# Weight tiles of the 256-column products placed alternately 64 and 192 bytes past the activations

## The chip, the core and the metric

The kernel runs on one core of one Trainium2 chip. The metric is the device time of one execution in microseconds (us), median of three runs; shorter is better. The core has a matrix engine (TensorE, in the profile PE for the products and PEld for the loads of their stationary operand), a vector engine (DVE), a scalar engine (ACT), a general engine (POOL, nearly unused here) and a queue that issues transfers (SP). All of them read and write an on-chip memory of 128 partitions. An address below is the byte offset in each partition, and only its remainder mod 256 matters to the change.

## The reference, cut to what matters

The reference is one layer of a decoder on 256 tokens of width 2048. It has two parts, and each ends in a layer norm of the residual sum:

```
h = layer_norm(x) * (1.0 + sc1) + sh1
y = token_mixer(h, w_in, ...)          # attention and mLSTM, merged, then @ w_o
x = layer_norm(ALPHA * x + g1 * y, ln_g[0], ln_b[0])
h = layer_norm(x) * (1.0 + sc2) + sh2
y = conv_ffn(h, w_up, ...)             # (silu(conv(h @ w_up[a])) * (h @ w_up[g])) @ w_down
x = layer_norm(ALPHA * x + g2 * y, ln_g[1], ln_b[1])
```

What matters for the change are two of the matrix products: `h @ w_in` for the part of the columns that is wanted transposed (3072 columns), and `h @ w_up` (2048 by 11264), the largest product of all.

## The kernel before, in words

Every large product is made of three products of split numbers. An fp32 weight tile `w` (128 x 1024) is loaded by the SP queue, ACT rounds it into `wh` (line 117), DVE forms the remainder `wl = w - wh` (line 118), and TensorE sums high times high, high times low and low times high. `wh` and `wl` come from a ring of four buffers each.

There are two forms. In the a-form (`mm_a`, lines 131 to 135) a block of activations is the stationary operand and the weights are streamed past it, 512, 392 or 256 columns at a time. In the b-form (`mm_b`, lines 125 to 129) a 128 x 128 block of the weight tile is the stationary operand, and 256 columns of activations (`hT` or `h2T`, high and low part) are streamed past it. Each product loads its stationary block anew, while the product before it is streaming. A weight tile of the b-form therefore gives 8 blocks and 24 products of 256 columns.

The b-form is used in two places:

- in the projection stage, by the stream `wb` over `w_in_b` (48 tiles, 1152 products, PSUM name `ps_b`). The contraction is cut into four groups of 3, 4, 5 and 4 blocks of 128 rows (`GROUPS`), so that the first products can start early. After the b-form products of a group come its a-form products (`ps_a`).
- in `up` (lines 1095 to 1117), over `w_up`: 44 values of `j`, each with four tiles (`b` for the two halves of the columns, `hf` for the two halves of the contraction), 176 tiles and 4224 products, PSUM name `ps_up`. The first 22 values of `j` run before the first half of the down projection, the other 22 after it.

TensorE takes its instructions in the order of the program; outside three short stretches that order is a scheduler's. `load_split(src, off)` takes a tile from each ring that is 1088 numbers wide (1024 + `OFFN`), and uses 1024 of them from number `off` on. A tile has 4352 bytes, 17 times 256, so that all four buffers have the same remainder, and `off` alone sets where the weights begin mod 256. The activations `hT` and `h2T` begin at remainder 0, and so does each block of 256 columns in them.

```
OFFB, OFFA, OFFN = 16, 48, 64      # line 41, in numbers of 4 bytes
```

Before, every b-form tile begins at number 16, 64 bytes past the remainder of the activations. The 256-column products of the a-form (in `proj_rows`, for `w_o` and `w_down`) use `OFFA`, 48 numbers or 192 bytes; there the weights are the streamed operand and the activations the stationary one, so that the stationary operand again begins 64 bytes (256 - 192) past the streamed one. The wider a-form products use no offset.

Of the kernel before, what the change touches and what calls it, by code (L numbers as in the profile page):

```python
# [14 lines left out]
P = 128  # L15
# [22 lines left out]
WB = (7, 4, 4)  # L38
NU0, NU1 = 4, 1
WARM = 20  # L40
OFFB, OFFA, OFFN = 16, 48, 64
MORD = (0, 2, 1, 3)
PTV = 2
YA = 2
# [1 line left out]
AW = 392  # L46
# [8 lines left out]
def build(ctx: ExitStack, tc: tile.TileContext, d, out, dbg=None):  # L55
# [36 lines left out]
    def t2(shape, name, dt=F32):  # L92
        return p0.tile(shape, dt, name=name, tag="t2", bufs=NT2)

    def bank(pool, name, dt=F32):
        return pool.tile([P, 512], dt, name=name, tag="b")

    def load(src):
        n = src.shape[-1]
        t = wp.tile([P, 1024], F32, name="w", tag="w", bufs=WB[0])  # L100
        nc.sync.dma_start(t[:, :n], src)
        return t
# [8 lines left out]
    def load_split(src, off=0):  # L111

        n = src.shape[-1]
        t = load(src)
        wh = wp.tile([P, 1024 + OFFN], F32R, name="wh", tag="wh", bufs=WB[1])[:, off:off + 1024]
        wl = wp.tile([P, 1024 + OFFN], F32R, name="wl", tag="wl", bufs=WB[2])[:, off:off + 1024]
        nc.scalar.copy(wh[:, :n], t[:, :n])  # L117
        lows.append(nc.vector.tensor_sub(wl[:, :n], t[:, :n], wh[:, :n]))  # L118
        return wh, wl
# [5 lines left out]
    def mm_b(ps, wh, wl, i, xt, k, start, stop):  # L125
        a, b = wh[:, i * P:(i + 1) * P], wl[:, i * P:(i + 1) * P]
        mm(ps, a, xt[:, k, 0, :], start, False)
        mm(ps, a, xt[:, k, 1, :], False, False)
        mm(ps, b, xt[:, k, 0, :], False, stop)
# [362 lines left out]

    def stream(src, width, per, off=0):

        tiles = iter(range(src.shape[0]))
        while True:
            wh, wl = load_split(src[next(tiles)][:, :width * per], off)
            work()
            for i in range(per):
                yield wh[:, i * width:(i + 1) * width], wl[:, i * width:(i + 1) * width]  # L500

    wb, wa, wv = (stream(d[n], w, p, o) for n, w, p, o in (("w_in_b", P, 8, OFFB), ("w_in_a", AW, 2, 0),
                                                           ("w_in_v", 512, 2, 0)))
    k0 = 0
    for gi, kn in enumerate(GROUPS):
        nxt = gi < len(GROUPS) - 1
# [7 lines left out]
        def work():  # L514
            if comp and next(comp[0], 1) is None:
                return
            comp.clear()
            tk.tick(rate)

        for b in range(NBLK):  # L520
            if b % 2 == 0:
                ps = bank(psm, "ps_b")
            for k in range(k0, k0 + kn):
                wh, wl = next(wb)
                mm_b(ps[:, (b % 2) * S:(b % 2 + 1) * S], wh, wl, 0, hT, k, k == k0, k == k0 + kn - 1)
            if b % 2 == 1:
                dst, kind = dest_b(b // 2)
                src = (ps.rearrange("p (w t k) -> p w t k", w=2, t=2) if kind
                       else ps.rearrange("p (a b) -> p a b", a=2))
# [9 lines left out]
        for c in range(6):  # L539
            pss = [bank(psm, "ps_a%d" % t) for t in range(2)]  # L540
            aw = AW if c < 4 else 512
            for k in range(k0, k0 + kn):
                wh, wl = next(wa if c < 4 else wv)
# [4 lines left out]
            for t in range(2):  # L548
                dst, src = projA[:, t, c * AW:(c + 1) * AW], pss[t][:, :aw]
                if c >= 4:  # L550
                    dst = mv1[:, t, 2 * c - 8:2 * c - 6, :MDV]
                    src = src.rearrange("p (h v) -> p h v", v=MDV)
# [469 lines left out]
    with tc.manual_schedule(engines={mybir.EngineType.DVE, mybir.EngineType.Activation}):  # L1022
# [33 lines left out]
        for p in range(8):  # L1056
# [8 lines left out]
            for i in range(2):  # L1065
                k = 2 * p + i
                src = pss[p // 2, i][:, (p % 2) * S:(p % 2 + 1) * S]
# [27 lines left out]
    def up(j):  # L1095

        ps = bank(psm, "ps_up")
        for b in range(2):
            for hf in range(2):
                wh, wl = load_split(d["w_up"][j * 4 + b * 2 + hf], OFFB)  # L1100
                for k in range(8):
                    mm_b(ps[:, b * S:(b + 1) * S], wh, wl, k, h2T, hf * 8 + k, hf == 0 and k == 0,
                         hf == 1 and k == 7)
                tk.tick(UR)
        a, gate = ps[:, :S], ps[:, S:]
        fw = lambda i: ffn[:, 3 * j + i:3 * j + i + 1]
        av = t2([P, S], "av")
        nc.scalar.activation(av, a, AF.Identity, bias=ffn[:, R_FB + j:R_FB + j + 1], scale=fw(2))
        for i in (1, 0):
            sh = 2 - i  # L1110
            nc.vector.scalar_tensor_tensor(av[:, sh:], a[:, :S - sh], fw(i), av[:, sh:],
                                           op0=ALU.mult, op1=ALU.add)
        nc.scalar.activation(av, av, AF.Silu)
        nc.vector.tensor_mul(av, av, gate)
        u = uTt[:, j % KH]
        nc.scalar.copy(u[:, 0, :], av)
        nc.vector.tensor_sub(u[:, 1, :], av, u[:, 0, :])

    for j in range(KH):
        up(j)  # L1120
        if j == 2:
            for c in range(2):
                tk.add(ada_rows(5, g2, c))
# [3 lines left out]
    for j in range(KH, KF):  # L1127
        up(j)
# [147 lines left out]
```

## Time and profile before

| what | value |
|---|---|
| median of 3 runs | 1485.79 us (1484.89, 1485.79, 1488.66) |
| the profiled execution, its own time | 1490.49 us |
| its span, first to last instruction | 1488.5 us |
| mean granted TensorE clock | 0.989 |
| TensorE busy (products) | 1439.5 us, 97% of the span |
| loads of stationary operands busy | 1304.1 us, 88% |
| DVE busy, ACT busy | 1072.4 us (72%), 710.0 us (48%) |
| DMA queue of the loads | 74.1% of the 16 engines' span |

A product is busy from its start until its last result, and the next one starts before that, so neighbouring products overlap. What a product costs in a dense stretch is therefore not its duration but the distance from one start to the next, called its pitch here. It is read from a timeline, where the starts stand, or from the number of products in a stretch that holds nothing else.

### The profile page before, as it was taken

The numbers are of one execution on the slowest core, as the hardware profiler recorded it, in microseconds if no ns is written. First come the engines' busy times: TensorE is split into PE (matmuls) and PEld (weight loads), VectorE is DVE, ScalarE is ACT, GpSimd is POOL, SyncE is SP. The second block draws the span as 40 slices with busy tenths as digits, with TensorE's granted clock in tenths as the row PEclk, the third lists the DMA queues.
The fourth block names the chain that finished last, engine by engine and source line by source line (L and its number), as shares of the span: only waits on it lengthen the run. The fifth ranks groups of instructions, "written<-read, shape, count | busy, mean of one in ns | idle before, by whom it ended". The sixth has DMA issues, their size and how long they took to land.

```text
span 1488.5 us, 24079 instructions
## 1 busy us (share of the span) xinstructions
PE 1439.5 (97%) x9470; PEld 1304.1 (88%) x9470; DVE 1072.4 (72%) x1565; ACT 710.0 (48%) x954; POOL 2.1 (0%) x6
## 2 busy tenths in 40 slices
PE   5999999999999999999699999999999999999997
PEld 4998998877667888888699999998899999999886
DVE  7899887888777798678867767755555555555566
ACT  5654443637764444435544444443334444444341
POOL 0000000000000000000000000000000000000000
PEclk9999999999999999999799999999999999999998
DMA  9999897885868999999078868866666666665661
GB/s 354 349 348 349 312 326 265 316 314 187 284 224 287 326 317 326 340 333 331 25 259 276 280 229 281 281 188 194 196 200 187 185 188 190 187 185 187 195 205 65
DMA packets 104081, 374.81 MB, mean 252 GB/s; under 512 B 11680, under 2 KB 12192, under 8 KB 103200
## 3 DMA queue, kind: packets, MB, share of 16 engines
q1 hardware_dynamic: 103968, 373.27, 74.1%
q8 instruction: 74, 1.21, 0.3%
q14 instruction: 39, 0.32, 0.1%
HBM read 371.13 MB, written 2.10 MB: 251 GB/s over the span
## 4 chain that ended last, share of the span: by engine, by line
PE 88%; DVE 6%; DMA 3%; ACT 2%; issue 1%; SPq 0%; DVEq 0%; ACTq 0%
PE ps_up L90 33%; PE ps_d L90 16%; PE ps_mg L90 10%; PE ps_b L90 7%; PE ps_br L90 6%; PE ps_a L90 6%; PE ps_o L90 5%; DVE wl L118 1%; DVE w L181 1%; PE ps_y L90 1%; DMA w<-in_w_in_b_dram 1%; DMA w<-in_w_in_v_dram 1%; ACT wh L117 1%; DVE xz L950 1%; DVE xz L955 1%
## 5 line engine op out<-in xcount | busy, mean ns | idle before, releaser
L118 DVE TENSOR_TENSOR wl<-w,wh 128x1024 fp32r<-128x1024 f32 (+1 forms) x478 | 576.3, 1206 | 350.3 <-ACT wh L117 348.4
L117 ACT CAST wh<-w 128x1024 fp32r<-128x1024 f32 (+1 forms) x478 | 495.3, 1038 | 657.3 <-PE ps_up L90 206.3
L90 PE MATMUL ps_up<-h2T,wh 128*128 128x256 f32 x2816 | 501.1, 282 | 0.5 <-DVE h2T L1077 0.3
L90 PEld LDWEIGHTS ps_up<-h2T,wh 128*128 128x128 f32 x2816 | 433.9, 189 | 1.0 <-DVE h2T L1077 0.5
L90 PE MATMUL ps_up<-h2T,wl 128*128 128x256 f32 x1408 | 396.3, 281 | 0.0
L90 PEld LDWEIGHTS ps_up<-h2T,wl 128*128 128x128 f32 x1408 | 268.0, 190 | 0.1
L181 DVE SCALAR_TENSOR_TENSOR w<-w,crow 128x1024 f32<-128x1024 f32 x192 | 233.6, 1219 | 1.1 <-DMA w<-in_w_ada_dram 1.1
L90 PE MATMUL ps_d<-wh,uTt 128*128 128x512 f32 (+1 forms) x792 | 209.8, 353 | 0.0
L90 PE MATMUL ps_mg<-wh,hT 128*128 128x512 f32 x512 | 169.9, 403 | 0.0
L90 PEld LDWEIGHTS ps_d<-wh,uTt 128*128 128x128 f32 x792 | 139.8, 188 | 20.7
L90 PE MATMUL ps_d<-wl,uTt 128*128 128x512 f32 (+1 forms) x396 | 139.8, 353 | 0.0
L90 PE MATMUL ps_b<-hT,wh 128*128 128x256 f32 x768 | 135.9, 282 | 2.7 <-ACT wh L117 2.7
L90 PEld LDWEIGHTS ps_b<-hT,wh 128*128 128x128 f32 x768 | 117.2, 190 | 7.2 <-issue 3.7
L90 PEld LDWEIGHTS ps_mg<-wh,hT 128*128 128x128 f32 x512 | 96.1, 188 | 23.5 <-issue 4.1
L90 PE MATMUL ps_a<-wh,hT 128*128 128x392 f32 (+1 forms) x384 | 110.6, 363 | 2.4 <-ACT wh L117 2.4
L90 PE MATMUL ps_b<-hT,wl 128*128 128x256 f32 x384 | 106.0, 281 | 0.6 <-DVE wl L118 0.5
L90 PE MATMUL ps_mg<-wl,hT 128*128 128x512 f32 x256 | 99.9, 390 | 0.0
L90 PEld LDWEIGHTS ps_d<-wl,uTt 128*128 128x128 f32 x396 | 74.4, 188 | 10.2
L90 PEld LDWEIGHTS ps_a<-wh,hT 128*128 128x128 f32 x384 | 71.5, 190 | 11.1 <-ACT wh L117 3.4
L90 PEld LDWEIGHTS ps_b<-hT,wl 128*128 128x128 f32 x384 | 72.6, 191 | 1.4 <-DVE wl L118 1.0
L90 PE MATMUL ps_a<-wl,hT 128*128 128x392 f32 (+1 forms) x192 | 69.4, 362 | 1.1 <-DVE wl L118 1.1
L90 PE MATMUL ps_o<-wh,mgT 128*128 128x512 f32 (+1 forms) x224 | 64.9, 374 | 0.0
(252 smaller groups left out, 1219.7 us busy)
## 6 DMA issues: line engine op xcount, KB each, us to landing
w<-in_w_ada_dram SPq DMA_DIRECT2D x192, 512.0 KB, 5.0
w<-in_w_up_dram SPq DMA_DIRECT2D x176, 512.0 KB, 4.2
w<-in_w_down_dram SPq DMA_DIRECT2D x90, 512.0 KB, 4.1
w<-in_w_mg_dram SPq DMA_DIRECT2D x64, 512.0 KB, 4.9
w<-in_w_in_b_dram SPq DMA_DIRECT2D x48, 512.0 KB, 5.3
w<-in_w_br_dram SPq DMA_DIRECT2D x32, 512.0 KB, 5.3
w<-in_w_o_dram SPq DMA_DIRECT2D x32, 512.0 KB, 4.8
w<-in_w_in_a_dram SPq DMA_DIRECT2D x32, 392.0 KB, 4.3
```

Of the source, the lines that this page charges most:

```text
L90: nc.tensor.matmul(o, lhsT, rhs, start=start, stop=stop)
L117: nc.scalar.copy(wh[:, :n], t[:, :n])
L118: lows.append(nc.vector.tensor_sub(wl[:, :n], t[:, :n], wh[:, :n]))
L181: ins = nc.vector.scalar_tensor_tensor(t, t, 1.0, crow[:, i * 1024:(i + 1) * 1024], op0=ALU.mult, op1=ALU.mult, accum_out=parts[:, row(m), ...
L950: nc.vector.scalar_tensor_tensor(z, z, mv[:, 0:1], lg[:, c * 512:(c + 1) * 512], op0=ALU.subtract, op1=ALU.mult)
L955: nc.vector.scalar_tensor_tensor(z, z, mv[:, 2:3], lb[:, c * 512:(c + 1) * 512], op0=ALU.mult, op1=ALU.add, accum_out=acc)
```

## The change

`OFFB` becomes a pair, and the tiles of the b-form take its two values in turn: 64 bytes past the activations' remainder for the even ones, 192 bytes for the odd ones. In `stream` the turn goes by the number of the tile in its array; in `up` it goes by `hf`, so that the tile of the first half of the contraction has 64 bytes and that of the second half 192. The streams `wa` and `wv` keep offset 0 and `OFFA` stays.

No instruction is added, taken away or moved on any engine; the loop of `stream` is written otherwise and gives the same sequence. What changes are addresses: half of the 224 b-form tiles (24 of `w_in_b`, 88 of `w_up`) move by 128 bytes inside their buffers, and with them 112 casts, 112 subtractions and 2688 products.

```
-OFFB, OFFA, OFFN = 16, 48, 64
+OFFB, OFFA, OFFN = (16, 48), 48, 64

     def stream(src, width, per, off=0):
-        tiles = iter(range(src.shape[0]))
-        while True:
-            wh, wl = load_split(src[next(tiles)][:, :width * per], off)
+        for i in range(src.shape[0]):
+            wh, wl = load_split(src[i][:, :width * per], off[i % 2])
             work()
             for i in range(per):
                 yield wh[:, i * width:(i + 1) * width], wl[:, i * width:(i + 1) * width]

-    wb, wa, wv = (stream(d[n], w, p, o) for n, w, p, o in (("w_in_b", P, 8, OFFB), ("w_in_a", AW, 2, 0),
-                                                           ("w_in_v", 512, 2, 0)))
+    wb, wa, wv = (stream(d[n], w, p, o) for n, w, p, o in (("w_in_b", P, 8, OFFB), ("w_in_a", AW, 2, (0, 0)),
+                                                           ("w_in_v", 512, 2, (0, 0))))

-                wh, wl = load_split(d["w_up"][j * 4 + b * 2 + hf], OFFB)
+                wh, wl = load_split(d["w_up"][j * 4 + b * 2 + hf], OFFB[hf])
```

## Rows read from the trace of the kernel before

**Rows 1.** The page: span, engines, chain by line, costliest products (busy, mean ns, idle).
```profile
span 1488.5 us, 24079 instructions
...
PE ps_up L90 33%; PE ps_d L90 16%; PE ps_mg L90 10%; PE ps_b L90 7%; PE ps_br L90 6%; PE ps_a L90 6%; PE ps_o L90 5%; DVE wl L118 1%; DVE w L181 1%; PE ps_y L90 1%; DMA w<-in_w_in_b_dram 1%; DMA w<-in_w_in_v_dram 1%; ACT wh L117 1%; DVE xz L950 1%; DVE xz L955 1%
...
L90 PE MATMUL ps_up<-h2T,wh 128*128 128x256 f32 x2816 | 501.1, 282 | 0.5 <-DVE h2T L1077 0.3
...
L90 PE MATMUL ps_up<-h2T,wl 128*128 128x256 f32 x1408 | 396.3, 281 | 0.0
```

**Rows 2.** Busy time by stage, two stretches of `up`; the first line names the columns.
```profile
core 0: us, PE busy (x) PEld busy (x) DVE busy (x) ACT busy (x) POOL busy (x), PEclk, DMA share, GB/s
...
745.00:875.00 130.00, 130.00 (x1107) 130.00 (x1106) 92.71 (x127) 62.76 (x82) 0.00 (x0) 1.00 0.78 263
1109.00:1355.00 246.00, 246.00 (x2091) 246.00 (x2091) 140.00 (x175) 114.04 (x150) 0.00 (x0) 1.00 0.62 187
```

**Rows 3.** Timeline of PE in `up` (start us, length us, product, count).
```profile
1199.75 0.28 PE L90 MATMUL ps_up<-h2T,wl 128*128 128x256 f32 x1
...
1200.11 0.28 PE L90 MATMUL ps_up<-h2T,wl 128*128 128x256 f32 x1
...
1200.81 0.28 PE L90 MATMUL ps_up<-h2T,wl 128*128 128x256 f32 x1
```

**Rows 4.** Timeline of PE in the projection stage, third group.
```profile
185.36 0.28 PE L90 MATMUL ps_b<-hT,wl 128*128 128x256 f32 x1
...
185.70 0.28 PE L90 MATMUL ps_b<-hT,wl 128*128 128x256 f32 x1
...
186.72 0.28 PE L90 MATMUL ps_b<-hT,wl 128*128 128x256 f32 x1
```

**Rows 5.** PE groups in 36:57, 84:112, 153:187, 694:714, 745:875, 1452:1476 us (busy, mean ns).
```profile
L90 PE MATMUL ps_b<-hT,wh 128*128 128x256 f32 x125 | 20.9, 276 | 0.0
...
L90 PE MATMUL ps_b<-hT,wh 128*128 128x256 f32 x160 | 28.4, 281 | 0.0
...
L90 PE MATMUL ps_b<-hT,wh 128*128 128x256 f32 x201 | 34.4, 276 | 0.0
...
L90 PE MATMUL ps_o<-hold,mgT 128*128 128x256 f32 x137 | 15.7, 276 | 0.0
...
L90 PE MATMUL ps_up<-h2T,wh 128*128 128x256 f32 x738 | 130.4, 281 | 0.0
...
L90 PE MATMUL ps_d<-hold,uTt 128*128 128x256 f32 x122 | 14.7, 281 | 0.0
```

**Rows 6.** Timeline of PE where 256-column products follow 512-column ones, `ps_b` and `ps_o`.
```profile
222.63 0.39 PE L90 MATMUL ps_a<-wh,hT 128*128 128x512 f32 x1
...
223.09 0.28 PE L90 MATMUL ps_b<-hT,wl 128*128 128x256 f32 x1
...
223.44 0.28 PE L90 MATMUL ps_b<-hT,wl 128*128 128x256 f32 x1
...
693.24 0.28 PE L90 MATMUL ps_o<-wl,mgT 128*128 128x256 f32 x1
...
693.60 0.28 PE L90 MATMUL ps_o<-wl,mgT 128*128 128x256 f32 x1
...
693.94 0.28 PE L90 MATMUL ps_o<-wl,mgT 128*128 128x256 f32 x1
```

**Rows 7.** Casts and subtractions of weight tiles in 745:875 and in 1445.5:1458 us.
```profile
L117 ACT CAST wh<-w 128x1024 fp32r<-128x1024 f32 x47 | 49.3, 1050 | 68.2 <-PE ps_up L90 54.6 <-issue 13.6
...
L118 DVE TENSOR_TENSOR wl<-w,wh 128x1024 fp32r<-128x1024 f32 x47 | 57.6, 1226 | 37.8 <-ACT wh L117 37.2
...
L117 ACT CAST wh<-w 128x1024 fp32r<-128x1024 f32 x4 | 4.2, 1043 | 0.0
...
L118 DVE TENSOR_TENSOR wl<-w,wh 128x1024 fp32r<-128x1024 f32 x4 | 4.9, 1220 | 0.0
```

**Rows 8.** What PE waited for from 30 to 300 us (total us, times, longest).
```profile
PE ps_b L90 <- ACT wh L117: 2.7, 1, 2.7
```

## The prediction

> **What bounds the kernel now.** I read the page first: its chain, then its costliest groups. The chain that ended last runs through TensorE, and 33% of the span are the `ps_up` products, which hardly ever find PE idle before them (0.5 us for the `wh` group, 0.0 for `wl`) [rows 1]. Then the stretches by stage: in 745 to 875 us and in 1109 to 1355 us, both inside `up`, PE and its weight loads are busy for the whole stretch, while DVE (92.7 of 130 and 140 of 246 us), ACT and the DMA engines (0.78 and 0.62) have room, at a granted clock of 1.00, the 2.4 GHz level [rows 2]. So in `up` the time is the number of products times their pitch, and nothing else stands in the way of a shorter pitch.
>
> Next the timelines, for the pitch itself. In `up` three groups of three products take 1200.81 - 1199.75 = 1.06 us, 117.8 ns each [rows 3]. In the third group of the projection four groups of three take 186.72 - 185.36 = 1.36 us, 113.3 ns each [rows 4]; for three products that is 353.3 against 340.0 ns. These are products of the same shape, at the same clock, with no wait, and in both the stationary operand begins 64 bytes past the streamed one. The same offset therefore goes with two steady pitches, 4.4 ns apart. The mean duration tells them apart in whole stretches: 281 ns goes with the long pitch, 276 ns with the short one. By that mark all of `ps_up` in 745 to 875 us is long, `ps_b` is long in 84 to 112 us and short in 36 to 57 and in 153 to 187 us, the last products of `w_o` are short and those of `w_down` long [rows 5].
>
> How a stretch enters decides which pitch it keeps. Behind 512-column products, without an idle moment, `ps_b` is at the long pitch within three products (223.44 - 223.09 = 0.35 us for three) and `ps_o` goes to the short one: 0.36 us for the first three, then 0.34 [rows 6]. I read this as two read streams of PE, the streamed operand and the next stationary block, which run side by side and settle into one of two phases to each other; a disturbance lets them settle anew. That reading is an inference: the rows show the two pitches and that an entry chooses between them, not why.
>
> **The change part by part.** No instruction is new and none moves. The casts and subtractions write 128 bytes further on in half of the tiles. Tiles with offset 192 exist already, in the 256-column products of `w_down`: a cast there takes 1043 ns against 1050 in `up`, a subtraction 1220 against 1226 [rows 7]. That is nothing, and if it were something, ACT and DVE have the room just named. The new loop of `stream` gives the same sequence: nothing.
>
> What is left is the pitch. The stationary block now begins 192 bytes past the streamed operand in half of the tiles, an arrangement that no product of 256 columns in this trace has, so its own pitch is not to be read. And at each change of tile the two streams are shifted against each other by 128 bytes, half of 256: a disturbance every 24 products, where `up` now runs for hundreds without one.
>
> The bounds: below, every product at the short pitch; above, the odd tiles at a pitch that is longer than any steady one seen. For that I take one more step of 4.4 ns, 122.2 ns, since the two steady pitches lie one such step apart.
>
> My forecast lies between. After each shift the products settle anew, and the stretches of this trace are short about as often as long (three and three in rows 5). All shifts of one kind are alike (24 products of steady pitch come before each), so I expect all tiles of one offset to end alike: one offset at 113.3 ns and the other at 117.8. Which one is which does not matter to the sum.
>
> - `up`: 88 tiles of 24 products gain 4.4 ns each: 88 x 24 x 4.44 = 9.4 us. Each has to settle first: by the entry of `ps_o` the first six products take 0.70 us where six at the short pitch take 0.68, so 0.02 us a tile, 1.8 us. Together -7.6 us.
> - `w_in_b`: here the first and third group (9 and 15 tiles) are short now and the second (12) is long [rows 5]; of the fourth (12) I take a quarter as long, for its entry [rows 6]. That is 33 tiles short and 15 long, an estimate from stretches carried over their groups. With 24 short ones, nine tiles lose 9 x 24 x 4.44 = +1.0 us, and settling costs 24 x 0.02 = +0.5 us. Waits for weights, 2.7 us for `ps_b` in the whole stage [rows 8], stay where they are. Together +1.4 us with rounding.
> - The 256-column products of `w_o` and `w_down` are not touched, but may enter otherwise than now: by the loops there are 528 for `w_down`, which at the short pitch would give 2.3 us back, and 192 for `w_o`, which at the long one would lose 0.9 us. I take nothing and keep both ends.
>
> The sum is -6.2 us, against the profiled execution's own 1490.5 us (its span of 1488.5 and 2.0 us around it). That execution was 4.7 us above the median of the runs shown. I take the difference from the median: 1485.8 - 6.2 = 1479.6 us. The runs differ by 3.8 us, which is about what 850 products at one pitch or the other make (850 x 4.44 ns); so a timed run may already have a stretch of `up` at the short pitch, and then less is left to gain.
>
> The place where the short pitch is hidden would be a stage in which weights come late. In `up` the loads use 0.62 to 0.78 of the DMA engines [rows 2], and 4% more products a microsecond need 4% more of that. There is no cover to lose.
>
> The Trainium skill speaks against an effect at all. Its page "SBUF — State Buffer", section "Who interferes with whom", gives PE two independent read ports, one for the streamed operand and one for the weight load, and says that PE never waits on anyone. By that rule the place of a weight tile changes no pitch, and the time stays at 1485.8 us. The trace does not show the cause of the two pitches, but it does show two where the rule leaves room for one; I weigh the rule as a rival below and not as the forecast.
>
> **The rivals.**
>
> *Every tile ends at the short pitch.* For it: `ps_o` gets there within three to six products of a disturbance, out of a dense stream [rows 6]. Against it: `ps_b` behind 222.63 us does not [rows 6], and no stretch of `up` in the rows did. Its sum: `up` gains 176 x 24 x 4.44 = 18.8 us less 176 x 0.02 = 3.5 us for settling, so -15.2; `w_in_b` gains 15 x 24 x 4.44 = 1.6 less 48 x 0.02 = 1.0, so -0.6. That is -15.8 us, 1470.0 us.
>
> *The change does nothing to the pitch.* Either the phase of the two streams has nothing to do with the remainder, or both offsets end at the pitch that they have now. For it: `up` sits at the long pitch in both halves, 117.8 ns in the second [rows 3] and 281 ns a product in the first [rows 5], so this may simply be what this loop has. Against it: the two pitches at one offset, which something has to choose. Its sum is 0, plus up to 0.01 us for each of 224 changes of tile, +2.2 us: 1485.8 to 1488.0 us.
>
> *The odd tiles are slower than any are now.* One mechanism, in one place: 192 bytes put the two streams where they meet more often, and 88 tiles of `up` run at 122.2 ns while the even ones stay at 117.8. For it: no row has this arrangement, and both forms of the 256-column product have the stationary operand 64 bytes past the streamed one, so nothing says that the other side is as good. Against it: nothing that the trace shows. Its sum: `up` 88 x 24 x 4.44 = +9.4 us and settling +1.8; `w_in_b` 24 tiles from a mean of 114.7 to 122.2 ns, 24 x 24 x 7.5 = +4.3. That is +15.5 us, 1501.3 us; with half a step, 120 ns, it is 4.7 + 1.8 + 3.1 = +9.6 us, 1495.4 us. It decides from a pitch of the odd tiles of about 119 ns on, if the even ones stay at 117.8; if the even ones turn short, only from 122 ns on.
>
> **How the numbers follow.** One offset short: 0.32. All short: 0.25. No effect: 0.17. Odd tiles slower: 0.26, of which I give a third to its milder forms, where even tiles turn short and the whole comes out near zero. What a measurement of this kernel can tell from no change is about 0.3%, 4.5 us. The forecast (-6.2 us with an own range of -9 to -3) gives 0.27 of its chance to faster and the rest to same; all short is faster; no effect is same. Faster 0.53, same 0.22, slower 0.25. The range reaches down to all short with the return of `w_down` (-15.8 - 2.3, 1468 us) and up to the half step of the slow rival (1495 us); beyond lie the full step above and little below. The forecast's own range is 1477 to 1483 us.
>
> **What would show it right or wrong.** In the timeline of `up` the distance of starts would go in steps of 24 products: 113.3 ns in tiles of one offset, 117.8 in those of the other, with three to six uneven products behind each change. The mean duration of `ps_up` products over the stage would lie between 276 and 281 ns. The number of products in 745 to 875 us would rise from 1107 to about 1125, and to about 1145 if every tile is short. Casts and subtractions would stay at 1050 and 1226 ns. Wrong would be: a single pitch in all of `up` (117.8 or 113.3), a duration above 281 ns in the odd tiles, or a gain that comes from a stage without b-form products.

## The result and the profile after

| | before | after |
|---|---|---|
| median of 6 timed runs each, side by side | 1487.22 us (1484.89 to 1491.93) | 1473.68 us (1471.91 to 1476.77) |
| the profiled execution, its own time | 1490.49 us | 1476.77 us |
| its span | 1488.5 us | 1474.8 us |

The ratio is 0.9909, with an interval of 0.989 to 0.9929: 13.5 us or 0.9% less, clear of the noise. That is inside the stated range (1468 to 1495 us), outside the forecast's own (1477 to 1483 us), and about twice the forecast of -6.2 us. The page of the kernel after, in the lines that answer to [rows 1]:

```profile
span 1474.8 us, 24079 instructions
...
PE ps_up L90 32%; PE ps_d L90 16%; PE ps_mg L90 11%; PE ps_b L90 8%; PE ps_br L90 6%; PE ps_o L90 5%; PE ps_a L90 5%; DVE w L181 1%; DVE wl L118 1%; DMA w<-in_w_in_v_dram 1%; PE ps_y L90 1%; ACT wh L117 1%; DVE xz L949 1%; DVE xz L954 1%; DMA w<-in_w_in_b_dram 1%
...
L90 PE MATMUL ps_up<-h2T,wh 128*128 128x256 f32 x2816 | 482.3, 277 | 0.5 <-DVE h2T L1076 0.3
...
L90 PE MATMUL ps_up<-h2T,wl 128*128 128x256 f32 x1408 | 389.1, 276 | 0.0
```

The chain is the same, with `ps_up` still in front of it; its products have gone from 282 and 281 ns to 277 and 276, as many and as little waited for. The stretches of [rows 2], again with all engines (PE, PEld, DVE, ACT, POOL, granted clock, DMA share, GB/s):

```profile
745.00:875.00 130.00, 130.00 (x1150) 130.00 (x1148) 95.54 (x131) 65.53 (x85) 0.00 (x0) 1.00 0.81 273
1109.00:1355.00 246.00, 246.00 (x2119) 243.87 (x2118) 144.28 (x179) 119.30 (x157) 0.00 (x0) 1.00 0.64 194
```

In the first of them 1150 products touch the 130 us, where there were 1107. 130 us at 113.3 ns are 1147; a window's count is two or three higher, since it holds every product that touches it. So the whole stretch is at the short pitch. (The second row runs past the end of `up` in this kernel, and its count is not to be compared.) The granted clock is 1.00 in both. PE takes more weights a microsecond, and the loads keep up: DMA goes from 0.78 to 0.81.

The timeline of PE shows the change of tile itself. At 765.40 us the offset goes from 64 to 192 bytes; at 883.45 us, behind 48 products at the long pitch, it goes from 192 to 64:

```profile
765.06 0.39 PE L90 MATMUL ps_up<-h2T,wh 128*128 128x256 f32 x2
...
765.40 0.39 PE L90 MATMUL ps_up<-h2T,wh 128*128 128x256 f32 x2
...
765.74 0.39 PE L90 MATMUL ps_up<-h2T,wh 128*128 128x256 f32 x2
...
766.08 0.39 PE L90 MATMUL ps_up<-h2T,wh 128*128 128x256 f32 x2
...
882.75 0.40 PE L90 MATMUL ps_up<-h2T,wh 128*128 128x256 f32 x2
...
883.10 0.40 PE L90 MATMUL ps_up<-h2T,wh 128*128 128x256 f32 x2
...
883.45 0.39 PE L90 MATMUL ps_up<-h2T,wh 128*128 128x256 f32 x2
...
883.79 0.39 PE L90 MATMUL ps_up<-h2T,wh 128*128 128x256 f32 x2
...
884.13 0.39 PE L90 MATMUL ps_up<-h2T,wh 128*128 128x256 f32 x2
```

Three products take 0.34 us on either side of 765.40: the step costs nothing, and both offsets run at 113.3 ns. At 883.45 three products go from 0.35 to 0.34 us with the first product of the new tile, and stay there. Behind its first products `up` is long in two places only, 48 products each: behind the eight small transposes (`ps_adar`, line 214) that interrupt it at about 877 us, and at the entry of its second half. The next step from 192 to 64 ends both.

Where the time went, by the starts of PE's products (first and last product of each stretch, from the timelines):

| stretch | before | after | difference |
|---|---|---|---|
| up to the first product of `up` | 730.14 us | 735.33 us | +5.2 |
| `up`, first half | 255.61 | 245.93 | -9.7 |
| from there to the second half (`w_down`) | 121.90 | 121.87 | 0.0 |
| `up`, second half | 248.63 | 239.46 | -9.2 |
| from there to the last product (`w_down`) | 120.88 | 120.88 | 0.0 |

The sum is -13.7 us, the difference of the two executions' own times (1476.77 - 1490.49). `up` alone gives 18.9 us; 5.2 us of it are lost before `up` begins.

Not all of the 18.9 us is pitch. Among the first 61 products of `up` are those that do not yet follow one another densely, and the granted clock is not yet 1.00 there. Windows of line 90 over them, of before and then of after (PE and PEld with their counts, granted clock, DMA share, GB/s):

```profile
730.10:743.30 13.20, 11.16 (x60) 9.47 (x61) 0.79 0.18 50
735.30:747.70 12.40, 10.38 (x60) 8.54 (x61) 0.85 0.18 53
```

This stretch is 0.8 us shorter in after, at a mean granted clock of 0.85 against 0.79. The dense rest gives 18.1 us, 8.9 in the first half and 9.2 in the second.

### The profile page after: what moved, and what is told of

Its sections match the earlier page's. It is cut to its first block, busy times and chain, and to the rows that moved or that the text cites. A ratio compares the mean times of both kernels' runs of the same rounds, so it can differ in the third digit from the quotient of the medians.

```text
span 1474.8 us, 24079 instructions
## 1 busy us (share of the span) xinstructions
PE 1424.0 (97%) x9470; PEld 1286.6 (87%) x9470; DVE 1071.9 (73%) x1565; ACT 711.0 (48%) x954; POOL 2.1 (0%) x6
## 4 chain that ended last, share of the span: by engine, by line
PE 88%; DVE 6%; ACT 2%; DMA 2%; issue 1%; SPq 0%; DVEq 0%; ACTq 0%
PE ps_up L90 32%; PE ps_d L90 16%; PE ps_mg L90 11%; PE ps_b L90 8%; PE ps_br L90 6%; PE ps_o L90 5%; PE ps_a L90 5%; DVE w L181 1%; DVE wl L118 1%; DMA w<-in_w_in_v_dram 1%; PE ps_y L90 1%; ACT wh L117 1%; DVE xz L949 1%; DVE xz L954 1%; DMA w<-in_w_in_b_dram 1%
## 5 line engine op out<-in xcount | busy, mean ns | idle before, releaser
L90 PE MATMUL ps_up<-h2T,wh 128*128 128x256 f32 x2816 | 482.3, 277 | 0.5 <-DVE h2T L1076 0.3
L90 PEld LDWEIGHTS ps_up<-h2T,wh 128*128 128x128 f32 x2816 | 425.1, 188 | 1.1 <-DVE h2T L1076 0.5
L90 PE MATMUL ps_up<-h2T,wl 128*128 128x256 f32 x1408 | 389.1, 276 | 0.0
L90 PEld LDWEIGHTS ps_up<-h2T,wl 128*128 128x128 f32 x1408 | 264.7, 188 | 0.1
```

The source lines that it names most:

```text
L90: nc.tensor.matmul(o, lhsT, rhs, start=start, stop=stop)
```

## The experiments

Edits are against the kernel after. Three theories stood at the start. A: it is the step, a change of the offset between two tiles, that takes the products out of the long pitch. B: 192 bytes is simply a better place than 64. C: every tile has to shift, because the products fall back without it.

A count in 70 us (790 to 860) is 620 at the short pitch and 597 at the long one; in 160 us (1140 to 1300) it is 1414 and 1361; in 30 us, 267 and 257. The rows below are windows for line 90 alone: PE and PEld with their counts, granted clock, DMA share, GB/s. A table behind the last experiment holds the times of all.

**Every tile at 192 (`c192`).**

```
-OFFB, OFFA, OFFN = (16, 48), 48, 64
+OFFB, OFFA, OFFN = (48, 48), 48, 64
```

> All b-form tiles begin at 192 bytes; no tile changes its offset. Theory A (a step out of the long pitch): the change helps because the step from a 192-byte tile to a 64-byte tile takes the streams out of the long pitch, and the short pitch survives both steps. With no step, `up` keeps what its entry gave, the long pitch of 117.8 ns (281 ns a product) over most of it, and the time is that of the kernel before within 5 us. Theory B (the better place): 192 bytes is the better place; `up` runs at 113.3 ns all through and the time is that of the changed kernel, 0.987 to 0.993 of the kernel before, or less.

```profile
790.00:860.00 70.00, 70.00 (x596) 70.00 (x596) 1.00 0.81 280
...
1140.00:1300.00 160.00, 160.00 (x1361) 160.00 (x1360) 1.00 0.60 186
```

All of `up` is at the long pitch, as before. The ratio is 1.0026 (1.0009 to 1.0042). B falls: the place alone gives nothing, and 192 bytes has a long phase too, the same 117.8 ns.

**One tile of 16 at 192 (`knock16`).** `w_in_b` stays at 64 throughout.

```
-                wh, wl = load_split(d["w_up"][j * 4 + b * 2 + hf], OFFB[hf])
+                wh, wl = load_split(d["w_up"][j * 4 + b * 2 + hf], 48 if (j * 4 + b * 2 + hf) % 16 == 1 else 16)
```

> `w_in_b` stays at 64 bytes, and in `up` only one tile in 16 (tiles 1, 17, 33, ...) begins at 192, 11 of 176. Theory A (a step out of the long pitch): one step from 192 to 64 is enough; `up` is at 113.3 ns from its third tile on, again at once after the interruption at about 878 us, and in its second half from tile 98 on, 10 tiles (1.1 us) later than in the changed kernel; `up` gains 16 to 18.5 us against the kernel before. Theory B (the better place): only the 11 tiles at 192 are short, `up` gains 1 to 2 us. Theory C (a shift at every tile is needed): short for at most a tile or two behind each step, `up` gains 1 to 4 us.

```profile
750.00:780.00 30.00, 30.00 (x257) 30.00 (x256) 1.00 0.70 228
790.00:860.00 70.00, 70.00 (x620) 70.00 (x619) 1.00 0.85 291
890.00:920.00 30.00, 30.00 (x257) 30.00 (x256) 1.00 0.83 282
925.00:955.00 30.00, 30.00 (x267) 30.00 (x267) 1.00 0.87 288
1140.00:1300.00 160.00, 160.00 (x1414) 160.00 (x1413) 1.00 0.63 194
```

The pitch changes at the steps back to 64 and keeps its level for 15 tiles at a constant offset. The first such step (745.53 us) changes nothing; the next (787.93) gives 113.3 ns, which holds until the interruption; the first behind that (921.07) gives it again. So C falls with B: one step can be enough, and the short phase holds by itself. In no execution at 64 and 192 bytes does the pitch of `up` change anywhere else than at an interruption or at a step from 192 to 64. `up` gains 13.7 us, less than expected, because a step does not always take. The ratio is 0.99 (0.9871 to 0.9929).

**Only `up` alternates (`up_only`).**

```
-    ... (("w_in_b", P, 8, OFFB), ...
+    ... (("w_in_b", P, 8, (16, 16)), ...
```

> The tiles alternate in `up` alone, `w_in_b` stays at 64 bytes. In the profile of the changed kernel `up` gained 18.9 us, and 5.2 us were lost before it, behind the projection, where nothing was changed. If that loss comes from the alternation in `w_in_b` (its products and so its transfers fall otherwise), it is gone here: `up` begins within 1 us of the kernel before, and the time is 4 to 6 us under the changed kernel's, a ratio to the kernel before of 0.986 to 0.989. If the loss varies from run to run whatever the kernel, the ratio is the changed kernel's, 0.989 to 0.993.

```profile
790.00:860.00 70.00, 70.00 (x620) 70.00 (x620) 1.00 0.84 289
...
1140.00:1300.00 160.00, 160.00 (x1414) 160.00 (x1413) 1.00 0.64 194
```

The gain is all in `up`: 18.4 us there in the profiled execution, ratio 0.9892 (0.986 to 0.9923), which is not to be told from the kernel after. Here too the first step (744.95) did not take, and the second (753.43) did.

**The kernel before once more, unchanged (`again_before`).**

> The kernel before, unchanged, for a second profile. Theory A says which pitch a stretch of `up` has is settled at its entry: the second profile may show a stretch at the short pitch that was long in the first (each half or part of `up` wholly one or the other, 4 to 10 us apart), and no tile in which the pitch changes without an interruption. If all of `up` is long again, the pitch is fixed by the program. The stage between the projection and `up` is expected to differ by some us if its 5.2 us vary from run to run, and by under 0.5 us if they are fixed by the program.

```profile
790.00:860.00 70.00, 70.00 (x620) 70.00 (x619) 1.00 0.84 285
890.00:920.00 30.00, 30.00 (x257) 30.00 (x257) 1.00 0.81 278
...
1140.00:1300.00 160.00, 160.00 (x1360) 160.00 (x1360) 1.00 0.62 186
```

The same program is short in the first part of `up`, where the profiled execution of before was long [rows 2], and long behind the interruption. The first half of `up` is 5.9 us shorter for it, 5.1 us by the pitch and 0.8 us in the first 61 products. So at a constant offset the entry decides the phase, and at the start of `up` it falls differently from run to run. The other two entries, behind the interruption and into the second half, came out long in every execution whose first tile there is at 64 or 192 (eleven and ten). At the start of `up`, the three executions at 64 and 192 whose granted clock stays at 0.5 for more than 5 us of it (before, `knock16`, `down128`) are long, and of the other seven (3.3 to 3.7 us) five are short; whether the one causes the other no run tests. This execution took 1483.90 us.

**Every tile at 0, and every tile at 128 (`c0`, `c128`).**

```
-OFFB, OFFA, OFFN = (16, 48), 48, 64
+OFFB, OFFA, OFFN = (0, 0), 48, 64        # c0
+OFFB, OFFA, OFFN = (32, 32), 48, 64      # c128
```

> All b-form tiles begin at the activations' own remainder, 0 bytes past it. If the remainder sets where the two streams meet, this place has steady pitches of its own, others than 113.3 and 117.8 ns; if the place is of no account to the pitch and only a step is, the two pitches are those of the kernel before, 276 and 281 ns a product.

> All b-form tiles begin 128 bytes past the activations' remainder. As for 0 bytes: pitches of its own if the remainder sets where the two streams meet, 113.3 and 117.8 ns (276 and 281 ns a product) if only a step counts.

The rows of `c0`:

```profile
790.00:860.00 70.00, 70.00 (x586) 70.00 (x585) 1.00 0.81 272
...
1140.00:1300.00 160.00, 160.00 (x1336) 160.00 (x1335) 1.00 0.60 183
```

The rows of `c128`:

```profile
790.00:860.00 70.00, 70.00 (x593) 70.00 (x592) 1.00 0.83 276
...
1140.00:1300.00 160.00, 160.00 (x1351) 160.00 (x1350) 1.00 0.60 186
```

The second half of `up` takes 253.31 and 250.50 us for 2111 distances: 120.0 and 118.7 ns. At 0 the products are evenly spaced; at 128 single ones lie between 115 and 122 ns apart.

**A step of 64 bytes (`step64`).**

```
-OFFB, OFFA, OFFN = (16, 48), 48, 64
+OFFB, OFFA, OFFN = (16, 32), 48, 64
```

> The tiles alternate between 64 and 128 bytes, a step of 64 instead of 128. If any step of the offset can take the streams out of the long pitch, `up` is at 113.3 ns after a few tiles behind each entry, as in the changed kernel (0.988 to 0.993 of the kernel before). If only some steps do, `up` keeps the long pitch in one or both of its halves (0.996 to 1.004). If 128 bytes is a worse place by itself, its tiles show a third pitch, above 118 ns, and the time is over that of the kernel before.

```profile
790.00:860.00 70.00, 70.00 (x604) 70.00 (x603) 1.00 0.84 285
...
1140.00:1300.00 160.00, 160.00 (x1379) 160.00 (x1378) 1.00 0.63 190
```

The step works as well as that of 128 bytes: behind a dense tile at 128 the tiles at 64 fall to 113 and 114 ns within four products (the first are 117, 123 and 118), mean 114.3 ns. But the tiles at 128 cost 118.2 ns, and most of the gain is gone: of the 9.2 us in the second half of `up` the profile keeps 3.2, and the times show none, ratio 1.0004 (0.9989 to 1.002). This is the pattern that the prediction drew, one offset short and the other long, at another pair of offsets.

**`w_down` alternates too (`down_too`).** `up` takes its pair in the other order.

```
-                    wh, wl = load_split(w[base + n], OFFA)
+                    wh, wl = load_split(w[base + n], OFFA if nm == "o" else OFFB[k0 // 4 % 2])
-                wh, wl = load_split(d["w_up"][j * 4 + b * 2 + hf], OFFB[hf])
+                wh, wl = load_split(d["w_up"][j * 4 + b * 2 + hf], OFFB[1 - hf])
```

> The changed kernel, with the 256-column tiles of `w_down` alternating as well (streamed weights at 64, then 192 bytes, so that the stationary operand is 192, then 64 bytes past the streamed one), and with the order of the two offsets in `up` reversed (192 first). Theory A (a step out of the long pitch): the step works in the a-form too; the 528 products of `w_down` at 117.8 ns in the changed kernel run at 113.3 from their second to fourth tile on, 1.5 to 2.3 us less in the last stage and behind the first half; after an interruption `up` is long for one tile, or three where the first step does not take, and not two. Together 2 to 3 us under the changed kernel, a ratio to the kernel before of 0.986 to 0.991. Theory D (only the b-form is moved by the step): `w_down` stays at 281 ns a product and the time is the changed kernel's.

```profile
1083.00:1100.00 17.00, 17.00 (x146) 17.00 (x146) 1.00 0.67 200
```

146 products touch the 17 us: `w_down` stays long. At a step one product is 114 ns from the next, and then the long pitch is back. In the a-form, where the weights are streamed, a step of 128 bytes does not take. `up` gains as much as with the other order.

**One tile of `w_down` at 128 in each half (`down128`).** The rest is the kernel after.

```
-                    wh, wl = load_split(w[base + n], OFFA)
+                    wh, wl = load_split(w[base + n], 32 if nm == "d" and c == 0 and k0 == 0 else OFFA)
```

> The changed kernel, and in `w_down` the first 256-column tile of each half 128 bytes apart instead of 64. If the step from 128 to 64 takes the a-form out of the long pitch as it does the b-form, the 256-column products of `w_down` run at 113.3 ns from the second tile on: 2 us under the changed kernel, a ratio of 0.987 to 0.992. If the a-form is not moved by it, as it was not by the step of 128 bytes, the ratio is the changed kernel's, 0.989 to 0.993, and these products stay at 281 ns.

```profile
1083.00:1100.00 17.00, 17.00 (x153) 17.00 (x152) 1.00 0.67 211
```

Now 153 touch the same 17 us. The tile at 128 costs 119.8 ns a product, and the 240 products behind it run at 113.4 ns. Each half of `w_down` is 1.0 us shorter: the second in the table, and the first by the time between the two halves of `up`, 120.88 us against 121.88. The median is 1469.17 us, ratio 0.9889 (0.9872 to 0.9905): the fastest kernel of this study, though its interval overlaps with that of the kernel after, so that the 2 us are shown by the trace and not by the times.

**Few steps, from 128 to 64 (`few128`).** All b-form tiles at 64 but tiles 2, 48 and 88 of `w_up` at 128; `w_down` as in `down128`.

```
-                wh, wl = load_split(d["w_up"][j * 4 + b * 2 + hf], OFFB[hf])
+                wh, wl = load_split(d["w_up"][j * 4 + b * 2 + hf], 32 if j * 4 + b * 2 + hf in (2, 48, 88) else 16)
```

> All b-form tiles at 64 bytes, but for three of `w_up` at 128: tile 2 (soon after the entry), tile 48 (behind the interruption) and tile 88 (first of the second half). In `w_down` the first 256-column tile of each half has its stationary operand 128 bytes past the streamed one, the others 64. In the run with 64 and 128 by turns every step from 128 to 64 ended at the short pitch. Theory A (a step out of the long pitch, which the short one survives): three steps do for `up`; all but about five of its tiles are at 113.3 ns, `up` gains 17.5 to 18.5 us against the first profile of the kernel before, and `w_down` 1.5 to 2.2 us more. Ratio to the kernel before 0.986 to 0.991. Theory C (each tile has to be shifted): nearly all of `up` as in the kernel before, 0.996 to 1.002.

```profile
790.00:860.00 70.00, 70.00 (x620) 70.00 (x619) 1.00 0.85 289
890.00:920.00 30.00, 30.00 (x257) 30.00 (x256) 1.00 0.78 276
...
1140.00:1300.00 160.00, 160.00 (x1360) 160.00 (x1360) 1.00 0.61 187
```

The first row looks as meant, but shows less than it seems to: before tile 2 begins, at 744.87 us, `up` is at the short pitch already, by its entry, as in `again_before`:

```profile
743.16 0.39 PE L90 MATMUL ps_up<-h2T,wh 128*128 128x256 f32 x2
...
743.50 0.39 PE L90 MATMUL ps_up<-h2T,wh 128*128 128x256 f32 x2
...
743.84 0.39 PE L90 MATMUL ps_up<-h2T,wh 128*128 128x256 f32 x2
```

So the steps behind tiles 2 and 48 show that the short pitch comes back behind a tile at 128, and not that they took `up` out of the long one. Tile 48 was misplaced besides: the interruption comes behind it, not before, so that nothing frees the products afterwards. Tile 88 is in its place, the first of the second half, and its step (1104.86 us) did not take: 2088 products stay long. That few steps are enough from 128 to 64 is therefore not shown. A single step may fail; in the kernel after the next one follows two tiles later. The ratio is 0.9984 (0.997 to 0.9997).

**Same remainder, other place (`rel0`).** Activations `h2T` and all tiles of `w_up` at 192, their distance 0.

```
-    h2T = big("h2T")
+    h2T = big("h2T", 48)
-                wh, wl = load_split(d["w_up"][j * 4 + b * 2 + hf], OFFB[hf])
+                wh, wl = load_split(d["w_up"][j * 4 + b * 2 + hf], 48)
```

(`w_in_b` is at 64, as before.)

> No alternation. `w_in_b` at 64 bytes as before; in `up` both the activations `h2T` and the weight tiles begin at 192 bytes, so that they are 0 bytes apart at a place where neither was in the kernel with all b-form tiles at 0. If only the distance of the two operands counts, `up` has the 120.0 ns that it had there (some 283 ns a product), and its 4224 products take 9 us more than at 117.8. If the weights' own remainder counts, `up` is at 117.8 or 113.3 ns as with all tiles at 192.

```profile
790.00:860.00 70.00, 70.00 (x585) 70.00 (x585) 1.00 0.81 274
...
1140.00:1300.00 160.00, 160.00 (x1336) 160.00 (x1335) 1.00 0.58 183
```

120.0 ns, as in `c0`. With weights at 192 and activations at 0 there are 117.8 ns (`c192`). So at distance 0 it is the distance between the two operands that counts, and not where either begins; the other distances were not tried at two places in the b-form.

**The kernel after once more, unchanged (`again_after`).**

> The changed kernel, unchanged, for a second profile. `up` is short but for at most four tiles behind each of its entries, as in the first profile; the stage between the projection and `up` differs from the first profile by 1 to 5 us if its loss varies from run to run, and by under 0.5 us if the change causes it.

```profile
790.00:860.00 70.00, 70.00 (x620) 70.00 (x619) 1.00 0.86 291
...
1140.00:1300.00 160.00, 160.00 (x1414) 160.00 (x1413) 1.00 0.64 194
```

`up` takes 245.93 and 239.46 us, to the hundredth as in the first profile of it. What the entry decides in the kernel before, the steps undo in this one. `up` begins 1.6 us earlier than in the first profile, so that the loss before it varies from run to run, in part at least.

All runs, from the profiled execution of each (starts of PE's products, us), with the median of the timed runs, or the one run (1). The medians of before that were timed beside them lie between 1486.42 and 1488.30 us.

| kernel | median | start of `up` | `up` 1st half | `up` 2nd half | end of `up` to last product |
|---|---|---|---|---|---|
| before | 1487.22 | 730.14 | 255.61 | 248.63 | 120.88 |
| again_before | 1483.90 (1) | 729.46 | 249.75 | 248.63 | 120.88 |
| after | 1473.68 | 735.33 | 245.93 | 239.46 | 120.88 |
| again_after | 1475.22 (1) | 733.77 | 245.93 | 239.46 | 120.88 |
| up_only | 1473.64 | 731.04 | 246.41 | 239.46 | 120.88 |
| knock16 | 1475.13 | 730.52 | 250.28 | 240.31 | 120.88 |
| down_too | 1473.27 | 734.48 | 246.02 | 239.37 | 120.88 |
| down128 | 1469.17 | 735.51 | 247.56 | 239.46 | 119.88 |
| few128 | 1484.49 | 731.11 | 250.04 | 248.64 | 119.88 |
| c192 | 1494.13 | 735.52 | 254.94 | 248.63 | 120.86 |
| step64 | 1488.40 | 730.37 | 252.90 | 245.48 | 120.87 |
| c128 | 1497.63 (1) | 734.26 | 256.77 | 250.50 | 120.87 |
| rel0 | 1498.83 (1) | 729.88 | 259.53 | 253.32 | 120.90 |
| c0 | 1507.48 (1) | 738.57 | 259.53 | 253.31 | 120.88 |

## Why the prediction was right, and where it was wrong

The time lies in the stated range because that was drawn wide enough to take in a rival, *every tile ends at the short pitch* (1470.0 us), and that rival is what happened in `up`. The forecast's own pattern did not come: by its own sign of being wrong, a single pitch of 113.3 ns in `up` (but for 96 products and the first few), it failed, and the 1150 products in 745 to 875 us answer to the rival's 1145 and not to its 1125.

**What bounds `up`: right.** Its time is the number of products times their pitch. 2111 distances at 117.78 ns are 248.63 us; 48 at 117.78 and 2063 at 113.33 are 239.45, against 239.46 measured. Nothing hid the gain and no load came late.

**Two phases, and an entry that chooses: right,** and shown more plainly by `again_before` than by the rows the prediction had. Why there are two stays open: the two read streams of the prediction are an inference that no run tests.

**"One offset at 113.3 ns and the other at 117.8": wrong.** This is the step that failed. The prediction took each change of tile as a new choice, with an end that depends on the offset. The runs show that the phase belongs to the run of products and not to the tile. In the six profiled executions that step between 64 and 192 in `up`, all steps met in the short phase (some 840, in both directions) kept it. In the long phase, with nine dense products ahead, 15 of 19 steps from 192 to 64 went to the short one, and none of 17 from 64 to 192 did. A step can free the products and does not trap them, so nearly all tiles end short. That is the rival that was given 0.25. Why only the one direction frees them stays open.

**Settling, 0.02 us a tile: wrong.** It costs nothing (765.40 us). The price was read from an entry behind 512-column products [rows 6], where the spacing itself changes; a step of offset in a dense run is no such entry. With both terms put right, 176 x 24 x 4.44 = 18.8 us for `up`. That the profile has 18.9 is partly chance: the pitch gives 18.1, since 96 dense products stay long and the first 61 are not counted in it, and 0.8 comes from that entry, nearly all by its clock. The two terms left out 9.4 and 1.8 us of gain.

**`w_in_b`, +1.4 us: wrong, though time is lost before `up`.** The mean durations go from 282 and 281 to 281 and 280 ns. Product by product, after is 0.4 us ahead at 273 us, and all products of `w_in_b` lie before 264 us. It falls back by 4.0 us between 285 and 320 us and by 1.7 us between 404 and 430 us, where no address was changed. Both stretches, two rows of before and then two of after (line 90):

```profile
290.00:312.00 22.00, 22.00 (x112) 18.12 (x111) 0.92 0.79 254
404.00:430.00 26.00, 22.69 (x82) 14.50 (x81) 1.00 0.61 211
290.00:312.00 22.00, 20.40 (x95) 16.52 (x94) 0.84 0.76 249
404.00:430.00 26.00, 22.88 (x78) 14.53 (x77) 0.93 0.65 234
```

The 1.7 us are the clock: its granted mean is 0.93 there against 1.00. They are not due to the change, since `again_before` has the same loss at the same 0.93. A third stretch of this kind costs 2.7 us in `again_after`, between 368 and 386 us (0.81 against 1.00 in before and after), and 2.6 to 2.8 us in five executions in which `w_in_b` doesn't alternate (`up_only`, `knock16`, `few128`, `c192`, `rel0`).

The 4.0 us seem to go with the change. There the granted mean is 0.84 against 0.92, and PE waits 0.9 us for ACT (`gT`) and 0.7 us for DVE (`sm`), which it does not in before. Against before, the four profiled executions in which `w_in_b` alternates between 64 and 192 lose 4.0 (after), 1.6 (`again_after`, at 0.84 too, without the waits), 2.7 (`down128`) and 4.2 us (`down_too`) in this stretch, and the five others with `w_in_b` at 64 nothing; but `c0` loses 1.6 us without alternating, and `step64`, alternating between 64 and 128, gains 1.0. Why the alternation should cost something behind its own products stays open; the medians of `up_only` and of after are the same (1473.64 and 1473.68 us), so that the times don't show it. The wait for `w_in_v` grew from 4.3 to 7.4 us in after, and is 2.4 us in `down_too`, which loses most: it is not that wait alone.

**Casts and subtractions: right,** no difference. In 745 to 875 us of after, against [rows 7]:

```profile
L118 DVE TENSOR_TENSOR wl<-w,wh 128x1024 fp32r<-128x1024 f32 x47 | 57.6, 1225 | 33.2 <-ACT wh L117 33.2
L117 ACT CAST wh<-w 128x1024 fp32r<-128x1024 f32 x48 | 50.4, 1051 | 63.4 <-PE ps_up L90 50.9 <-issue 12.5
```

**`w_down` and `w_o` untouched: right.** `w_down` is long before and after, 120.88 us to the hundredth, and `w_o` short (276 ns).

**The mark of 281 and 276 ns** for the two phases holds at 64 bytes but not everywhere: `c192` has 279 and 280 ns at the same long pitch. Starts, or counts in a window, are the safe reading.

**The rival "no effect".** The Trainium skill, "SBUF — State Buffer", section "Who interferes with whom", has PE's two read ports independent and PE waiting on no one. By that the place of a weight tile changes nothing. The measurements differ: 120.0, 118.7 and 113.3 or 117.8 ns with nothing but the distance of the two operands changed (`c0`, `c128`, after, `c192`; `rel0` for distance 0 at another place). **The rival "odd tiles slower"** had its price about right, and the wrong place: 120 ns is what distance 0 costs.

Not tried: taking the interruption at 877 us out of `up`, and a constant offset behind a sure first step.

## What to carry to other kernels

Where products run without a wait, read their pitch from starts, in more than one execution of the same program: a dense stream can sit in a slower steady state from its entry on, and at one entry here it was luck which. Then ask how far apart the two operands begin mod 256, and let that distance change now and then between two good values. It is the change that frees the stream (of the two here only the one from 192 to 64, and not each time), so it has to come again behind every interruption. Before putting a stretch down to the change, compare its granted clock too. When a mechanism has two states, ask of each event which of its transitions it can make, before giving every event a fair coin.

## What the runs showed of the hardware

- The pitch of the 256-column products of the b-form goes by the distance mod 256 from the streamed to the stationary operand: 120.0 ns at 0, 118.7 at 128, and at 64 and 192 either 113.3 or 117.8 ns. In the a-form, at 64, it has the same two values, and about 120 ns at 128. All at a granted clock of 1.00.
- The two phases hold for a thousand products and more at a constant offset (2088 long ones in `few128`, 1140 short ones in `again_before`). In the long one the distances repeat in threes (117, 118, 118 or 119), in the short one all are 113 or 114 ns.
- The b-form leaves the long phase by a step from 192 to 64 in 15 of 19 cases; the a-form (`w_down`) not by a step of 128 bytes, but it is at the short pitch behind a first tile at 128 in all four cases seen (`few128` and `down128`, both halves).
- The Trainium skill, "TensorE: Matmul & The Clock Gate", section "Back-to-back issue gap", gives 2.5 ns on top of the columns at 2.4 GHz for a product by itself, by which 256 columns would be 109.2 ns, an estimate; it adds that with weight loads both set the spacing. The shortest steady pitch here is 113.3 ns.
